# A batched matmul with masked softmax: 16 KB runs over four batches, and the mask in four blocks between the first loads

## The chip, the cores and the metric

The kernel runs on one core of a Trainium2 chip. The metric is the device time of one execution in microseconds. The median of 10 runs of the kernel before is 90.99 us (90.86 to 91.1).

## What is computed

For each of 16 batches a 512x512 matrix x is multiplied by one 512x512 weight matrix, scaled by 0.125, masked and put through a softmax along the rows:

```
y = scale * np.matmul(x, weight)
y = np.where(mask == 1, y, -1e9)
y_exp = np.exp(y - np.max(y, axis=-1, keepdims=True))
out = y_exp / np.sum(y_exp, axis=-1, keepdims=True)
```

The mask is 1 strictly below the diagonal and 0 elsewhere. A row i thus has weight on columns 0 to i-1 alone. Row 0 is masked throughout, so that all its 512 outputs are 1/512. All inputs and the output are fp32: x and the output have 16.8 MB each, the weight and the mask 1 MB each.

## The kernel before

**Units.** The work is cut into 16 units. A unit is one half (h = 0: rows 0 to 255, h = 1: rows 256 to 511) of two neighbouring batches, 512 rows in all. A partition holds four neighbouring rows, 8 KB in one run, so that 64 partitions hold one batch's half, and the two batches alternate from one partition to the next. The line that says it is `x_r = x.rearrange("(c e) (h p t) k -> c h p e (t k)", e=2, h=2, t=T)`, with T = 4. A load or a store moves one unit, 1 MB. Units alternate: even ones are upper halves and need only the first 256 output columns, odd ones need all 512.

**Steps of a unit.** `load` (L80) brings x on SP's queue. `cast` (L85, DVE) makes it bf16. `transpose` (L94, PE) puts 16 blocks of 128x128 into PSUM, and `evict` copies them out, one half on DVE (L104) and one on ACT (L105). `multiply` has, for each of four row slots t, four matmuls with the weight (L118), one matmul that adds the mask band (L127, an identity times a precomputed tile `band`, with -512 at masked places) and an exponential on ACT that also sums the row (L137). `normalise` takes the reciprocal (L152) and scales the rows (L154) on DVE, and for upper halves GpSimd writes 1/512 over row 0 (L156). `store` (L160) is issued on SP's queue. Output tiles of upper halves have their right-hand 256 columns zeroed once, ahead of the loop (L179), as they stay zero; row 0 gets its 1/512 there as well (L180).

**Mask.** Only the four diagonal 128x128 blocks of the mask are read, by one transfer of 256 KB in 512 runs of 512 B (L164). DVE turns them into 0 and -512 (L194). Four matmuls with a spreading matrix (L208) put them on the partitions of the unit layout, and DVE and ACT copy them into `band` (L215). The spreading matrix is made from the identity by ACT (L186), and the constant parts of `band` are filled by GpSimd (L176, L177).

**Order.** Nearly every instruction is inside `seq`, which keeps the order of the program text on each engine. SP's queue starts with load 0, the mask (L164), the weight (L165), and loads 1 to 7 (L167). There are 8 buffers for x and 8 for the output, 3 for xb and 3 for xt. PE first runs 12 dummy matmuls (L173). Then come, in this order, cast 0, the mask's arithmetic, transpose 0, evict 0, the band, the weight's casts (L216, L217) and cast 1. In step u of the loop (L220 on) stand transpose u+1, cast u+2, evict u+1, multiply u, normalise u-1, store u-1 and load u+7; PE thus reaches transpose 1 ahead of multiply 0.

Of the kernel before, what the change touches and what calls it, by code (L numbers as in the profile page):

```python
# [8 lines left out]
FP32 = mybir.dt.float32  # L9
BF16 = mybir.dt.bfloat16  # L10
AF = mybir.ActivationFunctionType
ALU = mybir.AluOpType

MASK_NEG = -512.0
P = 128
X_BUFS = 8
OUT_BUFS = 8
WARM = 12


@with_exitstack
def kernel(
    ctx: ExitStack,
    tc: tile.TileContext,
    x: bass.AP,
    weight: bass.AP,
    scale: float,
    mask: bass.AP,
    out: bass.AP,
):  # L30

    nc = tc.nc

    B, M, K = x.shape
    K2, N = weight.shape
    assert K == K2 and N == 512 and K == 512 and M == 512 and B % 2 == 0
    KT = K // P
    T = 4
    HP = P // 2
    HB = 2 * P
    U = B  # L50

    const = ctx.enter_context(tc.tile_pool(name="const", bufs=1))
    x_pool = ctx.enter_context(tc.tile_pool(name="xf", bufs=X_BUFS))
    xb_pool = ctx.enter_context(tc.tile_pool(name="xb", bufs=3))
    xt_pool = ctx.enter_context(tc.tile_pool(name="xt", bufs=3))
    sum_pool = ctx.enter_context(tc.tile_pool(name="sums", bufs=4))
    psum_t = ctx.enter_context(tc.tile_pool(name="psum_t", bufs=4, space=bass.MemoryType.PSUM))
    psum_y = ctx.enter_context(tc.tile_pool(name="psum_y", bufs=4, space=bass.MemoryType.PSUM))

    x_r = x.rearrange("(c e) (h p t) k -> c h p e (t k)", e=2, h=2, t=T)  # L60
    out_r = out.rearrange("(c e) (h p t) n -> c h p e (t n)", e=2, h=2, t=T)

    diag_r = bass.AP(tensor=mask.tensor, offset=mask.offset, ap=[[N, P], [P * N + P, KT], [1, P]])

    ident_bf = const.tile([P, P], BF16, name="ident_bf")
    w_f32 = const.tile([P, KT, N], FP32, name="w_f32")
    w_bf = const.tile([P, KT, N], BF16, name="w_bf")
    diag_f32 = const.tile([P, KT, P], FP32, name="diag_f32")
    diag_bf = const.tile([P, KT, P], BF16, name="diag_bf")
    spread = const.tile([P, T, P], BF16, name="spread")  # L70
    zeros = const.tile([P, N], BF16, name="zeros")
    band = const.tile([P, 2, T, HB], BF16, name="band")
    ots = [const.tile([P, T, N], FP32, name=f"ot{i}") for i in range(OUT_BUFS)]

    st_x, st_xb, st_pt, st_xt, st_sum = {}, {}, {}, {}, {}
    seq = tc.keep_in_program_order

    def load(u):
        xf = x_pool.tile([P, T, K], FP32, name="xf")
        seq(nc.sync.dma_start(xf.rearrange("p t k -> p (t k)"), x_r[u // 2, u % 2]))  # L80
        st_x[u] = xf

    def cast(u):
        xb = xb_pool.tile([P, T, K], BF16, name="xb")
        seq(nc.vector.tensor_copy(xb, st_x.pop(u)))  # L85
        st_xb[u] = xb

    def transpose(u):
        xb = st_xb.pop(u)
        st_pt[u] = [psum_t.tile([P, 2, T, P], BF16, name="pt") for _ in range(2)]  # L90
        for kt in range(KT):
            for t in range(T):
                seq(
                    nc.tensor.transpose(  # L94
                        st_pt[u][kt // 2][:, kt % 2, t],
                        xb[:, t].rearrange("p (k kt) -> p kt k", kt=KT)[:, kt],
                        ident_bf,
                    )
                )

    def evict(u):
        xt = xt_pool.tile([P, KT, T, P], BF16, name="xt")
        pt = st_pt.pop(u)
        seq(nc.vector.tensor_copy(xt[:, 0:2], pt[0]))  # L104
        seq(nc.scalar.copy(xt[:, 2:4], pt[1]))  # L105
        st_xt[u] = xt

    def multiply(u):
        h = u % 2
        NC = (h + 1) * HB  # L110
        xt = st_xt.pop(u)
        ot = ots[u % OUT_BUFS]
        rsum = sum_pool.tile([P, T], FP32, name="rsum")
        for t in range(T):
            py = psum_y.tile([P, N], FP32, name="py")
            for kt in range(KT):
                seq(
                    nc.tensor.matmul(  # L118
                        py[:, :NC],
                        lhsT=xt[:, kt, t],  # L120
                        rhs=w_bf[:, kt, :NC],
                        start=(kt == 0),
                        stop=(kt == KT - 1),
                    )
                )
            seq(
                nc.tensor.matmul(  # L127
                    py[:, h * HB : NC],
                    lhsT=ident_bf,
                    rhs=band[:, h, t],  # L130
                    start=False,
                    stop=True,
                    skip_group_check=True,
                )
            )
            seq(
                nc.scalar.activation(  # L137
                    out=ot[:, t, :NC],
                    in_=py[:, :NC],
                    func=AF.Exp,  # L140
                    bias=0.0,
                    scale=float(scale),
                    accum_out=rsum[:, t : t + 1],
                )
            )
        st_sum[u] = rsum

    def normalise(u):
        ot = ots[u % OUT_BUFS]
        NC = (u % 2 + 1) * HB  # L150
        rinv = sum_pool.tile([P, T], FP32, name="rinv")
        seq(nc.vector.reciprocal(rinv, st_sum.pop(u)))  # L152
        for t in range(T):
            seq(nc.vector.tensor_scalar_mul(ot[:, t, :NC], ot[:, t, :NC], rinv[:, t : t + 1]))  # L154
        if u % 2 == 0:
            seq(nc.gpsimd.memset(ot[0:2, 0, :HB], 1.0 / N))  # L156

    def store(u):
        ot = ots[u % OUT_BUFS]
        seq(nc.sync.dma_start(out_r[u // 2, u % 2], ot.rearrange("p t n -> p (t n)")))  # L160


    load(0)
    seq(nc.sync.dma_start(diag_f32, diag_r))  # L164
    seq(nc.sync.dma_start(w_f32, weight.rearrange("(p kt) n -> p kt n", kt=KT)))  # L165
    for u in range(1, X_BUFS):
        load(u)  # L167


    nc.vector.memset(zeros, 0.0)  # L170
    idle = psum_y.tile([P, N], FP32, name="py")
    for _ in range(WARM):
        seq(nc.tensor.matmul(idle, lhsT=zeros[:, :P], rhs=zeros, start=True, stop=True))  # L173

    make_identity(nc, ident_bf)
    nc.gpsimd.memset(band[:HP, :, :, P:], MASK_NEG)  # L176
    nc.gpsimd.memset(band[HP:, :, :, :P], 0.0)  # L177
    for i in range(0, OUT_BUFS, 2):
        nc.vector.memset(ots[i][:, :, HB:], 0.0)  # L179
        nc.gpsimd.memset(ots[i][0:2, 0, HB:], 1.0 / N)  # L180


    for g in range(2):
        for e in range(2):
            seq(
                nc.scalar.copy(  # L186
                    spread.rearrange("k t (g p e) -> k t g p e", g=2, e=2)[:, :, g, :, e],
                    ident_bf.rearrange("k (p t) -> k t p", t=T),
                )
            )  # L190

    cast(0)
    seq(
        nc.vector.tensor_scalar(  # L194
            out=diag_bf,
            in0=diag_f32,
            scalar1=-MASK_NEG,
            scalar2=MASK_NEG,
            op0=ALU.mult,
            op1=ALU.add,  # L200
        )
    )
    transpose(0)
    evict(0)
    for t in range(T):
        pm = psum_y.tile([P, N], FP32, name="py")
        seq(
            nc.tensor.matmul(  # L208
                pm, lhsT=spread[:, t], rhs=diag_bf.rearrange("k b c -> k (b c)"), start=True, stop=True
            )  # L210
        )
        for g, copy in enumerate((nc.vector.tensor_copy, nc.scalar.copy)):
            half = slice(g * HP, (g + 1) * HP)
            src = pm.rearrange("p (h g c) -> p h g c", h=2, g=2)
            seq(copy(band[half, :, t, g * P : (g + 1) * P], src[half, :, g]))  # L215
    seq(nc.vector.tensor_copy(w_bf[:, 0:2], w_f32[:, 0:2]))  # L216
    seq(nc.scalar.copy(w_bf[:, 2:4], w_f32[:, 2:4]))  # L217
    cast(1)

    for u in range(U + 1):  # L220
        if u + 1 < U:
            transpose(u + 1)
        if u + 2 < U:
            cast(u + 2)
        if u + 1 < U:
            evict(u + 1)
        if u < U:
            multiply(u)
        if u >= 1:
            normalise(u - 1)  # L230
            store(u - 1)
            if u - 1 + X_BUFS < U:
                load(u - 1 + X_BUFS)


# [33 lines left out]
```

The softmax here doesn't subtract the row's maximum and nothing guards it: scores larger than these inputs give would overflow.

## Time and profile before

| what | value |
|---|---|
| median of 10 runs | 90.99 us (90.86 to 91.1) |
| profiled execution | 91.0 us |
| its span, first to last instruction | 89.2 us |
| mean granted TensorE clock | 0.933 |
| busy: PE, DVE, ACT, POOL | 71.5, 60.4, 55.3, 7.3 us |
| DMA queue of the kernel: packets, MB | 5280, 34.87 |
| time that their packets took, share of 16 engines' span | 94.0% |
| mean over the span | 392 GB/s |
| median time from issue to landing: load, store, weight, mask | 14.1, 10.9, 8.5, 6.6 us |

The profile is that of one execution; its times count from the first instruction. PE is TensorE (PEld its weight loads), DVE is VectorE, ACT is ScalarE, POOL is GpSimd, SP is the engine that issues the transfers. A row of a timeline has the start, the length, the engine, the line and the operation, and in brackets how long the engine was idle before it and what ended that. A table by stretches of time gives for each stretch its length, the busy time of PE, PEld, DVE, ACT and POOL (with the instructions in brackets), the granted clock of TensorE, the mean busy share of the 16 DMA engines (packets are counted where they begin, so it can be a little over 1) and the rate in GB/s. The trace also holds a record of each DMA packet, and of each transfer's landing on each engine.

### The profile page before, as it was taken

What the parts mean: (1) busy time and instruction counts of PE and PEld (TensorE: products, weight loads), DVE (VectorE), ACT (ScalarE), POOL (GpSimd) and SP (SyncE); (2) the same over time, 40 slices, a digit from 0 to 9 for tenths busy, and PEclk for the clock granted to TensorE, in tenths of its full rate; (3) what the DMA queues carried; (4) which work ended last, traced back from release to release, by engine and by line L of the source; (5) the groups of instructions that cost most, each with busy time, mean ns of one, the idle gap of its engine ahead of it and who ended that gap; (6) DMA issues with size and microseconds to landing.
All of it is one profiled execution on the core that took longest, in us unless ns stands there. A gap on an engine that the chain in (4) does not pass through costs nothing.

```text
span 89.2 us, 1618 instructions
## 1 busy us (share of the span) xinstructions
PE 71.5 (80%) x592; PEld 49.2 (55%) x592; DVE 60.4 (68%) x123; ACT 55.3 (62%) x154; POOL 7.3 (8%) x20
## 2 busy tenths in 40 slices
PE   4976305999999999999999999999999999930000
PEld 1325005776598579649847965985697487500000
DVE  5866914758669949986994999599594966525000
ACT  5402930648777869687787877778787778650000
POOL 7620000002000200010020002002000200200000
PEclk9999975569999999999999999999999999999855
DMA  0969999999999999999999999999999999999970
GB/s 0 323 215 369 423 423 445 415 423 423 423 426 415 423 430 434 419 412 430 419 423 430 434 415 423 430 426 426 430 419 419 430 423 430 423 430 423 434 301 22
DMA packets 5286, 34.95 MB, mean 392 GB/s; under 512 B 544, under 2 KB 1056, under 8 KB 1056
## 3 DMA queue, kind: packets, MB, share of 16 engines
q1 hardware_dynamic: 5280, 34.87, 94.0%
q8 instruction: 4, 0.07, 0.3%
q14 instruction: 2, 0.02, 0.0%
HBM read 18.09 MB, written 16.78 MB: 391 GB/s over the span
## 4 chain that ended last, share of the span: by engine, by line
PE 72%; DMA 12%; DVE 3%; SPq 2%; ACT 1%; DVEq 0%; issue 0%; ACTq 0%
PE py L118 48%; PE pt L94 16%; DMA xf<-in_x_dram 12%; PE py L127 8%; DVE ot L154 1%; DVE xb L85 1%; SPq L80 1%; ACT ot L137 1%; SPq L164 1%; SPq L165 1%; DVEq L264 0%; DVE rinv L152 0%; ACTq L264 0%
## 5 line engine op out<-in xcount | busy, mean ns | idle before, releaser
L118 PE MATMUL py<-w_bf,xt 128*128 128x256 bf16 (+1 forms) x256 | 50.9, 333 | 0.0
L137 ACT ACTIVATE ot<-py 128x256 f32<-128x256 f32 (+1 forms) x64 | 31.2, 494 | 8.4 <-PE py L127 8.2
L118 PEld LDWEIGHTS <-xt 128*128 128x128 bf16 x256 | 25.1, 100 | 12.6
L105 ACT COPY xt<-pt 128x1024 bf16<-128x1024 bf16 x16 | 16.2, 1013 | 14.9 <-PE pt L94 10.4
L85 DVE CAST xb<-xf 128x2048 bf16<-128x2048 f32 x16 | 19.5, 1221 | 6.9 <-DMA xf<-in_x_dram 6.9
L154 DVE TENSOR_SCALAR ot<-ot,rinv 128x256 f32<-128x256 f32 (+1 forms) x64 | 23.5, 431 | 0.8
L94 PE MATMUL pt<-ident_bf,xb 128*128 128x128 bf16 x256 | 17.8, 225 | 6.0 <-DVE xb L85 6.0
L94 PEld LDWEIGHTS <-xb 128*128 128x128 bf16 x256 | 16.6, 115 | 7.9 <-DVE xb L85 7.0
L127 PE MATMUL py<-band,ident_bf 128*128 128x256 bf16 x64 | 17.8, 279 | 0.0
L104 DVE COPY xt<-pt 128x1024 bf16<-128x1024 bf16 x16 | 11.0, 688 | 7.8 <-PE pt L94 7.8
L137 ACT ACTIVATION_READ_ACCUMULATOR ot<-py 128x1 f32 x64 | 12.8, 200 | 0.0
L156 POOL MEMSET ot<- 2x256 f32 x8 | 3.6, 449 | 67.3 <-DVE ot L154 67.3
L127 PEld LDWEIGHTS <-ident_bf 128*128 128x128 bf16 x64 | 6.4, 100 | 4.3
L173 PE MATMUL py<-zeros 128*128 128x512 bf16 x12 | 4.9, 595 | 1.2 <-DVE zeros L170 1.2
L152 DVE RECIPROCAL rinv<-rsum 128x4 f32<-128x4 f32 x16 | 2.7, 169 | 3.2 <-ACT ot L137 3.2
L179 DVE MEMSET ot<- 128x1024 f32 x4 | 3.6, 912 | 0.6 <-issue 0.6
L173 PEld LDWEIGHTS <-zeros 128*128 128x128 bf16 x12 | 1.6, 144 | 3.9 <-issue 2.8
L186 ACT ACT_TABLE_LOAD x1 | 1.3, 1283 | 0.7 <-PEq L250 0.7
L215 DVE CAST band<-py 64x256 bf16<-64x256 f32 x4 | 1.4, 406 | 0.0
L215 ACT CAST band<-py 64x256 bf16<-64x256 f32 x4 | 1.3, 368 | 0.0
L180 POOL MEMSET ot<- 2x256 f32 x4 | 1.2, 302 | 1.5 <-DVE ot L179 1.4
L208 PE MATMUL py<-diag_bf,spread 128*128 128x512 bf16 x4 | 1.0, 377 | 0.2 <-DVE diag_bf L194 0.2
(14 smaller groups left out, 6.6 us busy)
## 6 DMA issues: line engine op xcount, KB each, us to landing
xf<-in_x_dram SPq DMA_DIRECT2D x16, 1024.0 KB, 14.1
out_dram<-ot SPq DMA_DIRECT2D x16, 1024.0 KB, 10.9
w_f<-in_weight_dram SPq DMA_DIRECT2D x1, 1024.0 KB, 8.5
diag_f<-in_mask_dram SPq DMA_DIRECT2D x1, 256.0 KB, 6.6
```

Source lines behind the costliest of these rows:

```text
L85: seq(nc.vector.tensor_copy(xb, st_x.pop(u)))
L94: nc.tensor.transpose(st_pt[u][kt // 2][:, kt % 2, t], xb[:, t].rearrange("p (k kt) -> p kt k", kt=KT)[:, kt], ident_bf,)
L104: seq(nc.vector.tensor_copy(xt[:, 0:2], pt[0]))
L105: seq(nc.scalar.copy(xt[:, 2:4], pt[1]))
L118: nc.tensor.matmul(py[:, :NC], lhsT=xt[:, kt, t], rhs=w_bf[:, kt, :NC], start=(kt == 0), stop=(kt == KT - 1),)
L127: nc.tensor.matmul(py[:, h * HB : NC], lhsT=ident_bf, rhs=band[:, h, t], start=False, stop=True, skip_group_check=True,)
L137: nc.scalar.activation(out=ot[:, t, :NC], in_=py[:, :NC], func=AF.Exp, bias=0.0, scale=float(scale), accum_out=rsum[:, t : t + 1],)
L152: seq(nc.vector.reciprocal(rinv, st_sum.pop(u)))
L154: seq(nc.vector.tensor_scalar_mul(ot[:, t, :NC], ot[:, t, :NC], rinv[:, t : t + 1]))
L156: seq(nc.gpsimd.memset(ot[0:2, 0, :HB], 1.0 / N))
L173: seq(nc.tensor.matmul(idle, lhsT=zeros[:, :P], rhs=zeros, start=True, stop=True))
L179: nc.vector.memset(ots[i][:, :, HB:], 0.0)
```

## The change

A group is now one half of four neighbouring batches, 2 MB. A partition holds eight neighbouring rows, a run of 16 KB; 32 partitions hold one batch's half, and four batches alternate. A group has two units: row slots 0 to 3 and 4 to 7. The order of units is therefore two upper, two lower, two upper and so on. There are 5 x buffers and 4 output buffers of 2 MB, and two buffers each for xb and xt.

Group 0 is loaded in two halves of 1 MB (8 KB runs); groups 1 to 7 are loaded whole. Groups 0 and 7 are stored in halves, groups 1 to 6 whole, after their second unit's normalise.

The mask's diagonal blocks come by four transfers of 64 KB, each to 16 partitions with eight neighbouring rows of 512 B. SP's queue starts with: first half of group 0, block 0, weight, block 1, second half of group 0, block 2, group 1, block 3, groups 2 to 4. The band is made in two parts, blocks 0 and 1 ahead of the first multiply, and blocks 2 and 3 after multiply 1; its tile has eight slots. Fourteen more dummy matmuls stand on PE behind transpose 0, and multiply 0 stands ahead of transpose 1.

```
-X_BUFS = 8
-OUT_BUFS = 8
+X_BUFS = 5
+OUT_BUFS = 4
...
-    xb_pool = ctx.enter_context(tc.tile_pool(name="xb", bufs=3))
-    xt_pool = ctx.enter_context(tc.tile_pool(name="xt", bufs=3))
+    xb_pool = ctx.enter_context(tc.tile_pool(name="xb", bufs=2))
+    xt_pool = ctx.enter_context(tc.tile_pool(name="xt", bufs=2))
...
+    x_r = x.rearrange("(c e) (h p t) k -> c h p e (t k)", e=E, h=2, t=S)
+    out_r = out.rearrange("(c e) (h p t) n -> c h p e (t n)", e=E, h=2, t=S)
...
+    def load(g, part=slice(0, S)):
+        if g not in st_x:
+            st_x[g] = x_pool.tile([P, S, K], FP32, name="xf")
+        run = slice(part.start * K, part.stop * K)
+        seq(nc.sync.dma_start(st_x[g].rearrange("p t k -> p (t k)")[:, run], x_r[g // 2, g % 2][:, :, run]))
...
+    def load_diag(b):
+        rows = slice(b * P, (b + 1) * P)
+        seq(
+            nc.sync.dma_start(
+                diag_f32[b * P // S : (b + 1) * P // S],
+                mask[rows, rows].rearrange("(p t) c -> p t c", t=S),
+            )
+        )
...
-    load(0)
-    seq(nc.sync.dma_start(diag_f32, diag_r))
+    load(0, slots(0))
+    load_diag(0)
     seq(nc.sync.dma_start(w_f32, weight.rearrange("(p kt) n -> p kt n", kt=KT)))
-    for u in range(1, X_BUFS):
-        load(u)
+    load_diag(1)
+    load(0, slots(1))
+    load_diag(2)
+    load(1)
+    load_diag(3)
+    for g in range(2, X_BUFS):
+        load(g)
...
     cast(0)
...
     transpose(0)
+    spin(14)
     evict(0)
...
     seq(nc.vector.tensor_copy(w_bf[:, 0:2], w_f32[:, 0:2]))
     seq(nc.scalar.copy(w_bf[:, 2:4], w_f32[:, 2:4]))
+    make_band(0)
     cast(1)
+    multiply(0)
+    transpose(1)
+    evict(1)

     for u in range(U + 1):
-        if u + 1 < U:
+        if 2 <= u + 1 < U:
             transpose(u + 1)
         if u + 2 < U:
             cast(u + 2)
-        if u + 1 < U:
+        if 2 <= u + 1 < U:
             evict(u + 1)
-        if u < U:
+        if 1 <= u < U:
             multiply(u)
+        if u == 1:
+            make_band(1)
         if u >= 1:
             normalise(u - 1)
-            store(u - 1)
-            if u - 1 + X_BUFS < U:
-                load(u - 1 + X_BUFS)
+            g, second = divmod(u - 1, 2)
+            if g in (0, G - 1):
+                store(g, slots(u - 1))
+            elif second:
+                store(g)
+            if second and g + X_BUFS < G:
+                load(g + X_BUFS)
```

`slots(u)` is the slice of row slots of unit u. `make_band(h)` does the mask's arithmetic on its two blocks (32 partitions, 1024 elements each), two matmuls with the spreading matrix, and after each a copy on DVE and one on ACT (64 partitions, 512 elements each). `spin(n)` issues n dummy matmuls of 512 columns.

## The prediction

> **What bounds the kernel now.** I read the page's slices first, then its DMA queues, then the chain. The chain puts 72% on PE, which would make TensorE the bound; the slices say something else.
>
> ```profile
> PE   4976305999999999999999999999999999930000
> DMA  0969999999999999999999999999999999999970
> GB/s 0 323 215 369 423 423 445 415 423 423 423 426 415 423 430 434 419 412 430 419 423 430 434 415 423 430 426 426 430 419 419 430 423 430 423 430 423 434 301 22
> DMA packets 5286, 34.95 MB, mean 392 GB/s; under 512 B 544, under 2 KB 1056, under 8 KB 1056
> q1 hardware_dynamic: 5280, 34.87, 94.0%
> ```
>
> PE is idle in the last four slices while the DMA engines go on at 423 to 434 GB/s. From the fifth slice to the 37th they are full at one rate, whether loads, stores or both are moving. Two early slices (215 and 369) are poor. The packets are 544 semaphore writes (34 transfers x 16 engines), 512 mask rows of 512 B, and 4224 of 8 KB. Next, stretches of time: busy columns first, the last two numbers are DMA share and GB/s.
>
> ```profile
> 5.00:5.50 0.50, 0.50 (x3) 0.21 (x2) 0.43 (x1) 0.00 (x0) 0.01 (x1) 1.00 0.81 324
> 5.50:6.00 0.50, 0.50 (x3) 0.09 (x1) 0.00 (x0) 0.00 (x0) 0.29 (x1) 1.00 0.50 127
> 6.00:6.50 0.50, 0.10 (x1) 0.00 (x0) 0.45 (x1) 0.00 (x0) 0.00 (x0) 1.00 0.50 136
> 6.50:7.00 0.50, 0.00 (x0) 0.00 (x0) 0.50 (x1) 0.00 (x0) 0.00 (x0) 1.00 0.33 54
> 7.00:7.50 0.50, 0.16 (x3) 0.17 (x4) 0.28 (x1) 0.00 (x0) 0.00 (x0) 1.00 0.98 320
> ...
> 70.00:80.00 10.00, 8.86 (x66) 5.60 (x64) 5.83 (x19) 7.40 (x23) 0.90 (x2) 1.00 1.01 426
> 80.00:82.00 2.00, 0.00 (x0) 0.00 (x0) 1.51 (x4) 0.00 (x0) 0.00 (x0) 1.00 1.00 422
> 82.00:84.00 2.00, 0.00 (x0) 0.00 (x0) 0.00 (x0) 0.00 (x0) 0.00 (x0) 1.00 1.02 430
> ```
>
> From 5.4 to 7.2 us the engines move the mask and stand idle half of that time; nowhere else between 3.4 and 85 us is there such a hole. Third, the end and the loads. The last row is the last store; the two casts wait for consecutive 1 MB loads.
>
> ```profile
> 13.07 1.23 DVE L85 CAST xb<-xf 128x2048 bf16<-128x2048 f32 x1 [1.79 <-DMA xf<-in_x_dram]
> 15.55 1.23 DVE L85 CAST xb<-xf 128x2048 bf16<-128x2048 f32 x1 [1.26 <-DMA xf<-in_x_dram]
> ...
> 81.54 0.54 SPq L160 DMA_DIRECT2D out_dram<-ot  x1
> ```
>
> The last store is issued at 81.54 and its landings, one for each engine, run from 86.07 to 88.19. The landings of the store ahead of it run from 83.64 to 85.76, 2.43 us earlier at both ends: each engine went from one to the other without a pause. So **the slowest DMA engine's list of packets sets the end**. A store that met an empty queue would need 81.54 + 1.46 (issue to first packet, from 0.74 to 2.20 for the first load) + 2.43 + 0.75 (receipt) = 86.2. PE, whose last matmul ends at 78.87, thus has 2.0 us to spare.
>
> [...] The trace runs at 423 to 430[...] its packet records have medians of 309 ns for 8 KB, 27 for 512 B and 9 for the semaphore writes, so 282 ns for 7680 B, or 27.2 B/ns, and about 8 ns a packet whatever its size. Check: 8 packets of 309 and one of 9 are 2.48 us, and 15.55 - 13.07 is 2.48. [...] Here it fell at 12.4 us, after PE had nothing from 9.6 on, and came back at 19.2.
>
> **The change, part by part.** The profiled execution took 91.0 us (span 89.2 and 1.8 around it); the median of the runs is 90.99, so one sum serves both.
>
> *16 KB runs.* Each engine carries 8 packets of a load or store. Loads 1 to 7 and stores 1 to 6 become 2 MB with 16 KB runs: 13 x 8 = 104 packets in place of 208. By the fit a packet of 16 KB takes 8 + 16384/27.2 = 610 ns against 618 for two, say 7 to 8 ns saved, 0.75 us per engine. Group 0 and the stores of group 7 stay at 8 KB. [...] the fit has no 16 KB data packet in it, so I allow a loss too, up to +1.7 (16 ns more than two small ones), see the rivals. I take **-0.75**.
>
> *Fewer transfers.* 34 become 24 (9 loads, 10 stores, 4 mask blocks, the weight): 10 semaphore writes of 9 ns per engine, **-0.09**. SP's issue time, about 0.6 us each, is off the path: SP has long waits for the normalise (57.5 us in all) and has issued the first ten transfers by 8.6 us, while their data last until 22. Now the first nine transfers, through the 2 MB load behind the last mask block, are issued by about 6 us.
>
> *Mask in four blocks.* 512 rows of 512 B before and after, 32 per engine, busy 32 x 27 = 0.86 us either way. What can go is the hole: 5.4 to 7.2 us is 1.8 us, so 0.9 idle. Before, 32 small packets follow on each engine; now 8, with a megabyte on either side. Best, the hole is gone, -0.9. Worst, a quarter of it comes back at each block, 0 (a loss beyond that has no ground: the bytes and rows are the same). The records show 512 B packets in two bursts of about 16 per engine with a gap from 6.4 to 6.8 us; 8 are half a burst, so I take **-0.65**.
>
> *Starting order.* Multiply 0 is moved ahead of transpose 1, and the loads of group 1 come as 2 MB. Landings, from the first load's 6.03: block 0 about 6.3, weight 9.0 (before 10.57), block 1 9.3, second half of group 0 11.8, group 1 17.0. The 14 added dummy matmuls sit on PE ahead of the band and multiply 0. At the 0.22 us that a warm 128x512 matmul takes they end at 8.42 + 3.0 = 11.5, some 0.9 us after the band's input is ready: that is their price, covered because PE then waits anyway. Band: two matmuls, then two casts on each of DVE and ACT, twice as wide as the 406 and 368 ns rows, 1.3 us; multiply 0 runs from 12.1 to 14.5; cast 1 is behind the band casts on DVE, 14.3; transpose 1 ends at 15.5. Transpose 2 stands ahead of multiply 1 on PE and needs cast 2, so the 2 MB load: 17.0 + 1.2 = 18.2. PE idles for 2.7 us.
>
> *From there to PE's end.* Units of 256 columns take 0.89 + 2.18 = 3.07 us of PE, of 512 columns 4.77 (chain). From 18.2: 14 transposes at 0.89, seven narrow and eight wide multiplies (15.3 + 31.0), the second band 0.5: 59.3, so 77.5, against 78.87 before. If the clock falls in the wait, add up to 2.4 (half of 12.4 to 19.2 that PE was busy, from 14.36). DVE per narrow unit has 1.22 + 0.69 + 0.17 + 1.27 = 3.35 us, 0.3 more than PE, twice running; the wide units (3.75 of 4.77) give that back, and an eviction has 1 to 2 us before PE needs it. Later loads are early: group 5, issued about 28.4, lands near 42 and is used at 50; group 7 near 62 for use at 65.7.
>
> *Stores.* One 2 MB store for two units leaves up to 4.8 us later than its first half did. Cover: queued work. Store 5 is issued about 65 and the queue holds until 70; store 6 about 71 against 75; the two halves of group 7 at 76 and 80.1 against 81 and 83.6. The last has 83.6 - 80.1 - 1.5 = 2.0 us. Without cover its delay would add one for one. The wider DVE and POOL fills at the start are the same bytes and end before 6 us. Halving xb and xt to two buffers costs nothing: each is read, in PE's order, before its next writer. The dropped x buffers matter no more, as 10 MB are still ahead.
>
> **Sum**: -0.75 - 0.09 - 0.65 = -1.5; 91.0 - 1.5 = **89.5 us**. The slowest engine's last packet then ends near 85.9 in place of 87.4.
>
> **The rivals.** (1) *Only one half works*: runs of 16 KB are as slow as two of 8 KB, 90.3, or the hole comes back block by block, 90.2. For it: no 16 KB data packet was seen, and what limits small packets isn't shown. (2) *Compute takes over.* The mask gains nothing, group 1 lands at 17.9, PE idles for 3.7 us and its clock falls for 4.8: PE ends at 78.4 + 2.4 = 80.8, the last store leaves at 83.5 and lands at 88.1 as before: 90.9. Against: the dummies, and 2.0 us of room. (3) *Slower: 16 KB runs move worse.* Place: each of 104 packets on each engine. Price: 16 ns over two small ones is 104 x 16 = 1.7 us, less 0.74 of the other parts: 91.9. It decides from 7 ns on. For it: the only 16 KB packets in the trace, four of the instruction queue, took 945 to 1024 ns, far over 618, and four batches stand a megabyte apart. Against: those shared their engine with the data queue[...]. (4) *All goes to its best end*: [...] below 88.9 the last store's own path would be the bound.
>
> **How the numbers follow.** A measurement of this kernel tells about 0.2% (0.2 us). Chances: forecast (89.2 to 90.0) 57%, one half 18%, compute 8%, slower 12%, best end 5%. Faster 0.80, same 0.08, slower 0.12. Range 88.9 to 90.9: it leaves out the slower case and part of the compute case.
>
> **What would show it.** Right: no slice under 380 GB/s after the first two; plain rate up one per cent, to about 428 to 430; engines still full when PE has stopped; last store issued near 80. Wrong: DMA share below 0.9 before 83 us (compute), a half-clock stretch at 17 to 22 us, packets over 618 ns, or a dip at each of the four blocks.

## The result, and the profile after

The changed kernel takes 93.51 us (median of 9 runs, 92.31 to 94.17) against 90.98 for the kernel before: a ratio of 1.0225, 95% interval 1.0201 to 1.0249. Slower by 2.2%, where 89.5 was forecast. The ratio leaves out executions more than 1.5% above a kernel's fastest (here two, 93.73 and 94.17), so it is below 93.51 / 90.98 = 1.028, and differences from the changed kernel are taken from the ratios below, 0.01 being 0.91 us. Its profiled execution took 93.62 us with a span of 91.8.

First the page's slices: TensorE, its granted clock, the DMA engines and their rate, and the packets.

```profile
PE   4965968305999999999999999999999999993000
PEclk9999999965589999999999999999999999999955
DMA  0969999999999999999999999999999999999691
GB/s 0 378 189 399 321 360 385 403 340 407 435 421 435 407 417 417 457 421 393 432 439 421 421 357 400 435 435 435 414 435 435 414 414 393 400 428 400 250 417 61
DMA packets 3462, 34.95 MB, mean 381 GB/s; under 512 B 384, under 2 KB 896, under 8 KB 896
```

The packets are as forecast: 384 semaphore writes, and the 8 KB packets mostly gone. The rate is not. From the third slice to the ninth (4.6 to 21 us) 380 GB/s and more were forecast; four of the seven show 189, 321, 360 and 340, where the plain rate is some 425. TensorE has a gap in the eighth slice to the tenth and then half its clock. And near the end there is a slice of 250 GB/s that the kernel before didn't have. The first weakness in steps of half a microsecond (the last two columns are DMA share and GB/s):

```profile
5.00:5.50 0.50, 0.50 (x3) 0.25 (x2) 0.42 (x1) 0.00 (x0) 0.24 (x2) 1.00 1.31 211
5.50:6.00 0.50, 0.49 (x3) 0.00 (x0) 0.00 (x0) 0.00 (x0) 0.28 (x1) 1.00 0.15 58
6.00:6.50 0.50, 0.00 (x0) 0.00 (x0) 0.00 (x0) 0.00 (x0) 0.00 (x0) 1.00 0.40 157
6.50:7.00 0.50, 0.00 (x0) 0.00 (x0) 0.48 (x1) 0.00 (x0) 0.00 (x0) 1.00 0.55 229
...
9.50:10.00 0.50, 0.50 (x4) 0.20 (x2) 0.00 (x0) 0.44 (x1) 0.00 (x0) 1.00 0.83 198
...
12.50:13.00 0.50, 0.50 (x4) 0.14 (x3) 0.26 (x1) 0.00 (x0) 0.00 (x0) 1.00 0.84 219
...
18.00:18.50 0.50, 0.00 (x0) 0.00 (x0) 0.00 (x0) 0.00 (x0) 0.00 (x0) 1.00 1.34 308
18.50:19.00 0.50, 0.00 (x0) 0.00 (x0) 0.00 (x0) 0.00 (x0) 0.00 (x0) 1.00 0.80 214
```

The rows at 5.0 to 6.5, at 9.5, at 12.5 and at 18 to 19 us are the places where a mask block has just passed. Each is a dip in the rate, and the kernel before has only one, though its mask came in one piece of four times the size. But only the first dip is idle time. The table counts a packet where it begins; counted over the packets' whole lengths, the engines are idle for about half of 5.5 to 6.5, and hardly at all in the other three places. There the packets themselves take longer: those of 16 KB that begin between 12 and 14 us have a median of 932 ns, and 611 over the whole run. From 4 to 25 us, each engine spends 2.7 us more in its packets than their usual lengths come to (the run's medians for each size), in the kernel before 0.3. It is idle for 0.7 us there, in the kernel before for 0.9. So most of the loss at the start is slow packets. The expectations below call all four places holes.

What PE makes of it, in the timeline:

```profile
15.85 1.06 PE L98 MATMUL pt<-ident_bf,xb 128*128 128x128 bf16 x16
20.43 2.36 DVE L89 CAST xb<-xf 128x2048 bf16<-128x2048 f32 x2 [3.24 <-DMA xf<-in_x_dram]
21.71 1.90 PE L98 MATMUL pt<-ident_bf,xb 128*128 128x128 bf16 x16 [4.81 <-DVE xb L89]
...
30.16 3.52 SPq L165 DMA_DIRECT2D out_dram<-ot  x2
```

PE finishes transpose 1 at 16.9. Cast 2 needs group 1, which lands at 20.34 on its slowest engine (17.0 was forecast), so PE stands idle for 4.8 us. Its granted clock falls to half at 19.0 and is back at 25.8 (in the kernel before it was at half from 12.4 to 19.2); the 16 transposes at 21.71 take 1.90 us in place of 1.06. The first store goes out at 30.2, in the kernel before at 22.6. The last one leaves at 86.1, as the last start in its row says:

```profile
L165 SPq DMA_DIRECT2D out_dram<-ot x10: 538/548/621, 30.2 to 86.1; - x10
```

That is late enough for the queue to run dry, in the table of stretches at the end:

```profile
85.00:86.00 1.00, 0.00 (x0) 0.00 (x0) 1.00 (x3) 0.00 (x0) 0.00 (x0) 1.00 0.93 385
86.00:87.00 1.00, 0.00 (x0) 0.00 (x0) 0.07 (x1) 0.00 (x0) 0.00 (x0) 1.00 0.33 139
87.00:88.00 1.00, 0.00 (x0) 0.00 (x0) 0.00 (x0) 0.00 (x0) 0.00 (x0) 0.64 0.84 352
88.00:89.00 1.00, 0.00 (x0) 0.00 (x0) 0.00 (x0) 0.00 (x0) 0.00 (x0) 0.50 1.06 434
```

From 86 to 87 the engines are a third busy, then the last 1 MB moves. By the landing records most of the 16 engines waited; the slowest went from the last store but one (landed at 88.56) to the last (91.01) in 2.45 us, without a pause. The last landing stands 0.36 us behind the end of the last packet (90.65), in the kernel before 0.47 (88.19 behind 87.72), where the forecast had 0.75 for the receipt. So two things end together here: PE's work, and the list of the slowest DMA engine.

### The profile page after: what moved, and what is told of

The parts are those of the page before. It is cut to its first block, busy times and chain, and to the rows that moved or that the text cites. A ratio compares the mean times of both kernels' runs of the same rounds, so it can differ in the third digit from the quotient of the medians.

```text
span 91.8 us, 1619 instructions
## 1 busy us (share of the span) xinstructions
PE 74.6 (81%) x606; PEld 50.1 (55%) x606; DVE 61.8 (67%) x122; ACT 56.0 (61%) x154; POOL 6.6 (7%) x14
## 4 chain that ended last, share of the span: by engine, by line
PE 67%; DMA 17%; SPq 4%; DVE 3%; ACT 1%; issue 1%; DVEq 0%; ACTq 0%
PE py L122 44%; DMA xf<-in_x_dram 17%; PE pt L98 15%; PE py L131 7%; SPq L172 2%; DVE ot L158 1%; SPq L85 1%; DVE xb L89 1%; ACT ot L141 1%; SPq L181 1%; PE py L226 1%; DVEq L305 0%; DVE rinv L156 0%; ACTq L305 0%; DVEq L89 0%
## 5 line engine op out<-in xcount | busy, mean ns | idle before, releaser
L109 ACT COPY xt<-pt 128x1024 bf16<-128x1024 bf16 x16 | 16.2, 1013 | 15.7 <-PE pt L98 11.5
L158 DVE TENSOR_SCALAR ot<-ot,rinv 128x256 f32<-128x256 f32 (+1 forms) x64 | 23.0, 423 | 0.7
L89 DVE CAST xb<-xf 128x2048 bf16<-128x2048 f32 x16 | 19.5, 1221 | 4.8 <-DMA xf<-in_x_dram 4.8
L196 PE MATMUL py<-zeros 128*128 128x512 bf16 x26 | 8.0, 473 | 1.2 <-DVE zeros L191 1.2
L160 POOL MEMSET ot<- 4x256 f32 x4 | 1.8, 448 | 66.8 <-DVE ot L158 66.8
L196 PEld LDWEIGHTS <-zeros 128*128 128x128 bf16 x26 | 2.9, 117 | 5.3 <-issue 2.7
L237 DVE CAST band<-py 64x512 bf16<-64x512 f32 x4 | 2.6, 678 | 3.5 <-PE py L226 3.5
L204 DVE MEMSET ot<- 128x2048 f32 x2 | 3.5, 1765 | 0.8 <-issue 0.8
L237 ACT CAST band<-py 64x512 bf16<-64x512 f32 x4 | 2.3, 582 | 2.0 <-DVE band L237 2.0
L247 DVE CAST w_bf<-w_f 128x1024 bf16<-128x1024 f32 x1 | 0.7, 695 | 1.8 <-DMA w_f<-in_weight_dram 1.8
L202 POOL MEMSET band<- 64x2048 bf16 x1 | 1.8, 1801 | 0.1
L201 POOL MEMSET band<- 64x2048 bf16 x1 | 1.8, 1803 | 0.0
```

The lines of the kernel that those rows point to most:

```text
L89: seq(nc.vector.tensor_copy(xb, st_x[u // 2][:, slots(u)]))
L237: copy(band[half, h, slots(j), g * P : (g + 1) * P], pm.rearrange("p (t c) -> p t c", t=T)[half],)
```

## The experiments

I held three theories. **A**: each short mask transfer opens a hole in the DMA queue, which delays all that follows. **B**: PE's order is at fault, as transpose 2 waits for a whole 2 MB load and the clock falls. **C**: 16 KB runs over four batches are served worse. Numbers in brackets are ratios to the kernel before, with 95% intervals.

### The mask left out (e1)

```
-        seq(nc.sync.dma_start(diag_f32[...], mask[rows, rows]...))
+        if b == 0:
+            nc.gpsimd.memset(diag_f32, 1.0)
```

> The changed kernel without its four mask transfers (the blocks are filled with ones on GpSimd, so the mask is left out of the computation). Theory A (each 64 KB block opens a hole of about 1 us in the DMA queue; that delays every engine's list and group 1): no slice under 380 GB/s after the first two, group 1 lands near 17 us, the engines' spread at the start falls below 1 us, PE ends near 78, about 90.0 us. Rival B (compute order: transpose 2 waits for a whole 2 MB load, and the clock falls): PE still waits over 4 us at half clock, 92.5. Rival C (16 KB runs over four batches drive the engines apart): rate and spread as in the changed kernel, 92.3 or more.

90.43 us (0.995, 0.9925 to 0.9975): 2.5 us less than with the mask, by the ratios. Group 1 lands at 15.67 with the engines within 0.4 us, PE waits 1.5 us for it, the clock stays up, and the first store leaves at 23.9.

```profile
17.35 1.08 PE L98 MATMUL pt<-ident_bf,xb 128*128 128x128 bf16 x16 [1.47 <-DVE xb L89]
23.86 3.50 SPq L165 DMA_DIRECT2D out_dram<-ot  x2
```

Rival C is out: with the same 16 KB runs the spread at the start is gone. The cause lies with the four transfers, a quarter of a megabyte out of 35.

### Group 1 in halves (e2), and the clock kept up (e3)

```
-    load(1)
-    load_diag(3)
+    load(1, slots(0))
+    load_diag(3)
+    load(1, slots(1))
```

> The changed kernel with group 1 loaded as two transfers of 1 MB, block 3 between them. Theory A: unit 2 can start some 2 us earlier, but the slowest DMA engine's list is as long as before, so 93.0 to 93.5. Rival B (PE's start sets the time): PE ends near 81, about 91. Rival C: 93.5.

```
     transpose(1)
+    spin(20)
     evict(1)
```

> The changed kernel with 20 more dummy matmuls behind transpose 1, which keep TensorE's clock up while it waits for group 1. Theory A: PE ends about 2 us earlier, near 81.5, but the slowest engine's list stays, 93.0 to 93.4. Rival B: the clock was the loss, 91.5. Rival C: 93.5.

e2 took 92.26 us (1.0149, 1.0084 to 1.0213), e3 91.73 (1.0087, 1.0066 to 1.0108). Each was less than A had said and more than B had, e3 only by a little. In e3 the clock never falls while work is left:

```profile
PEclk9999999999999999999999999999999999999555
```

Both undo a consequence, and each gets back part. In e2 PE ends at 79.2 and the last store leaves at 81.9, 4.2 us earlier than in the changed kernel, yet it lands only 1.2 us earlier, at 89.79: there the slowest engine's list is the end. So neither A nor B alone: the blocks lengthen the DMA list, and by way of group 1 they start PE late and cold. Either one holds the end up when the other is mended.

### The kernel before with four blocks (e4)

```
-    seq(nc.sync.dma_start(diag_f32, diag_r))
+    seq(nc.sync.dma_start(diag_f32[:, 0:1], diag_r[:, 0:1]))
     seq(nc.sync.dma_start(w_f32, ...))
+    (block 1, load 1, block 2, load 2, block 3)
```

> The kernel before with its mask in four transfers of 64 KB (one diagonal block each, on 128 partitions), the first second in the queue, then one behind the weight, one behind load 1 and one behind load 2; all else is the kernel before. Theory A: three more holes of about 1 us at the start, 93 to 94. Rivals B and C: nothing of theirs is in it, 90.5 to 91.0.

94.60 us (1.0388, 1.035 to 1.0425), a little more than A had said. But the trace shows another reason, so this supports nothing. All four blocks gate this kernel's band, and the fourth lands at 15.04: DVE waits 8 us for it, and the first store leaves at 26.9.

```profile
15.16 0.43 DVE L203 TENSOR_SCALAR diag_bf<-diag_f 128x512 bf16<-128x512 f32 x1 [7.97 <-DMA diag_f<-in_mask_dram]
26.94 0.61 SPq L160 DMA_DIRECT2D out_dram<-ot  x1
```

Meanwhile the clock is down. The stores come late, so that the queue is empty from 27 to 28 us, where no packet begins; the rate stays uneven until 40:

```profile
PEclk9999965556999999999999999999999999999855
GB/s 28 308 404 361 358 418 421 436 418 432 414 202 340 290 436 358 305 382 436 407 439 407 443 421 418 421 436 421 428 428 414 439 411 439 414 432 414 390 315 21
```

And where A expected three more holes there are none: load 3 lands at 17.49, in the kernel before at 18.02. These blocks have the same bytes and the same runs of 512 B as those of the changed kernel. What differs is where they land: 128 partitions with one row each, in place of 16 partitions with eight.

### What in a block opens the hole (e5, e6, e8)

e5 keeps place and size of the blocks but moves 4 KB runs, to 16 partitions (mask left out); e6 issues the real blocks on ACT's queue; e8 is the changed kernel again.

```
+        seq(nc.sync.dma_start(side[b], mask[32 * b : 32 * b + 32].rearrange("(p t) c -> p (t c)", t=2)))
```

> The changed kernel with each of its four mask transfers replaced by one of the same 64 KB at the same place in the queue, but in 16 runs of 4 KB in place of 128 runs of 512 B; they go to a tile that nothing reads, and the blocks are filled with ones on GpSimd (so the mask is left out of the computation). Theory A1 (any short transfer opens the hole[...]): holes as before, 92.5 to 93.5. Theory A2 (the 512 B runs are what is slow): about the kernel without the mask plus 0.6 us for 256 KB, 91.0.

```
-            nc.sync.dma_start(
+            nc.scalar.dma_start(
```

> The changed kernel with its four mask transfers issued on ACT's queue in place of SP's, all at the start. Theory A1: beside the loads on SP's queue they open no hole between loads; only their packets cost time, 91.0 to 91.4. Theory A2: the 512 B runs cost the same on any queue, 92.5 to 93.5.

> The changed kernel once more, unaltered, for a second profile beside the others of this batch. If the holes vary from run to run, group 1 lands anywhere from 18.3 us (as with the added dummies) to 20.4 (as in the first profile), and the time goes with it, 92.3 to 94.2; if the dummies had a hand in the early landings, 20 us and 93.5 again.

e5: 92.57 us (1.0174, 1.0155 to 1.0192), group 1 at 18.80. So it isn't the 512 B runs. e6: 92.39 (1.0148, 1.0104 to 1.0191), group 1 at 19.17. So it isn't the place in SP's queue either; on ACT's queue the blocks trickle in beside the loads for up to 17 us:

```profile
DMA to landing us min/median/max: 6.3/10.5/17.1
```

e8: 92.82 (1.0198, 1.0154 to 1.0241), group 1 at 19.15. What the blocks cost varies from run to run, so that single profiles of this kernel differ by more than a microsecond; the earlier landing in e3 (18.35) may be more of the same. A1, that any short transfer does it, still stood after these three, but e4 spoke against it.

### The kernel before without its mask (e7)

```
-    seq(nc.sync.dma_start(diag_f32, diag_r))
+    nc.gpsimd.memset(diag_f32, 1.0)
```

> The kernel before without its mask transfer (blocks filled with ones on GpSimd, the mask left out of the computation). It gives the price of the mask in the kernel before and, against the changed kernel without its mask (90.4), what the rest of the change is worth. If the mask cost 1.8 us there, 89.2, and the rest of the change loses 1.2. If runs of 16 KB pay as forecast (0.75), 91.2 would have to come out, which leaves the mask no price at all; in between, the rest of the change is worth the difference.

90.33 us (0.9928, 0.9905 to 0.9951). Load 3 lands 1.9 us earlier (16.10), but only 0.65 arrives at the end. The rate falls short while the last of the first loads are under way (the first store is issued at 19.5, the second at 23.5 us):

```profile
24.00:25.00 1.00, 1.00 (x13) 0.65 (x11) 1.00 (x2) 0.54 (x2) 0.00 (x0) 1.00 1.10 295
25.00:26.00 1.00, 1.00 (x7) 0.52 (x6) 0.96 (x5) 1.00 (x3) 0.28 (x1) 1.00 0.88 320
```

The engines are not idle there; over their whole length the packets fill these two microseconds. Again they take longer: of the 75 packets of 8 KB that begin there 26 take over 430 ns, where 309 is usual. With that the slowest engine falls back: one load lands from 22.90 to 24.66 on the 16 engines, the next from 25.83 to 28.61. At the end the first engine is done 1.4 us earlier than in the kernel before (84.70 against 86.07), the slowest only 0.7 (87.49 against 88.19). So a gain in the first loads isn't all kept: the slowest engine's lag takes a part of it, and my sum had no such term. Why packets slow down there isn't shown; e1 has the same from 27 to 31 us, 1.2 us per engine.

Against e1 (90.43 us, 0.995) this run also prices the rest of the change: without the mask it is worth nothing, where 0.84 us had been forecast for it.

### Where the blocks land (e9, e10)

Both leave the mask out and move its blocks, at their places, to a tile that nothing reads.

```
e9:  nc.sync.dma_start(side[b], mask[rows, rows])
e10: nc.sync.dma_start(side[b][::8], mask[rows, rows].rearrange("(p t) c -> p t c", t=S))
```

> The changed kernel with its four mask transfers replaced by four of the same bytes (128 runs of 512 B, same place in the queue) that go to 128 partitions with one row each, in place of 16 partitions with eight rows each. They go to a tile that nothing reads, and the blocks are filled with ones on GpSimd (the mask is left out of the computation). Theory D (what opens the hole is that a block lands on 16 neighbouring partitions[...]): blocks cost 0.35 us each, group 1 lands at 16.5 to 17.0 with the engines within 1 us, 90.5 to 91.0. Theory A1 (any short transfer): group 1 at 18.5 to 20, 92.5.

> As the kernel with 128 partitions (mask left out likewise), but each block goes to 16 partitions that lie eight apart, with eight rows each. Theory D: [...] less than half of the excess, group 1 at 17.0 to 17.8, 91 to 92. Theory A1, or a theory in which it is the eight rows to a partition: as in the changed kernel, group 1 at 18.5 or later, 92.5.

e9: 90.99 us (0.9993, 0.9978 to 1.0008), group 1 at 17.61. e10: 92.08 (1.0137, 1.0102 to 1.0173), group 1 at 18.47. With 16 neighbouring partitions it is 92.57 with the mask left out likewise (e5), 93.51 and 92.82 with it. Same bytes, same places in the queue, equally short: that a block is short (A1) is not the cause of the excess. Theory D, the place where a block lands, holds for 128 partitions in the time, though group 1 comes 0.6 us later than it said. For 16 spread ones, where "less than half of the excess" was my estimate, the order is right, but the times don't decide: e10 lies just beyond the slow end of what D said, its range (91.84 to 92.83) touches that of the neighbours (from 92.31), and the rival with eight rows to a partition had put group 1 at 18.5.

The lengths of the packets separate them better. From 4 to 25 us they exceed the usual, per engine, by 2.7, 1.9 and 2.4 us with 16 neighbours (the changed kernel, e8, e5), by 1.3 with 16 spread partitions (e10), by 0.6 with 128 (e9; also e11 and e12), and by 0.2 with no block at all (e1). As e10 has as many partitions, and as many rows to each, as the changed kernel, how far apart they lie matters by itself (1.3 us against 1.9 to 2.7), as far as single profiles tell.

From e10 to e9 the number of partitions changes along with their distance, and no run here shows what it is in the place that makes the packets longer.

### The blocks on 128 partitions, with the whole computation (e11, e12, e13)

```
-                diag_f32[b * P // S : (b + 1) * P // S],
-                mask[rows, rows].rearrange("(p t) c -> p t c", t=S),
+                diag_f32[:, b : b + 1], mask[rows, rows]...
...
-        for j in range(2):
+        for t in range(S):
             ... lhsT=spread[:, t], rhs=diag_bf[:, 2 * h : 2 * h + 2] ...
```

> The changed kernel with each mask block loaded to 128 partitions, a row to each, at the same places in the queue, and the band made from that (eight matmuls of 256 columns and sixteen casts of 128 columns in each half). The computation is whole. Theory D: group 1 lands near 16.7, PE waits about 2 us less than in the changed kernel, PE ends near 79, 90.7 to 91.4. Theory A1: 92.5 or more.

e12 and e13 add `spin(10)` behind transpose 1.

> The same with ten more dummy matmuls behind transpose 1, so that the clock cannot fall while PE waits for group 1. Theory D: the wait is short enough without them, so within 0.3 us of the kernel without the ten, 90.5 to 91.2. Theory A1: 91.7, as the changed kernel with dummies.

> The kernel with 128-partition mask blocks and ten dummies again, as the measure for the two others: 90.3 to 90.7, under the kernel before by 0.4 to 0.6 us.

e11: 90.98 us (1.0004, 0.9982 to 1.0025). e12: 90.49 (0.9954, 0.9934 to 0.9974), e13: 90.53 (0.9948, 0.993 to 0.9965). Behind the first block of e12 there is no hole, and group 1 lands at 17.12, where the prediction had it at 17.0 (17.59 in e11, whose own expectation was 16.7):

```profile
5.00:6.00 1.00, 1.00 (x4) 0.30 (x2) 0.50 (x2) 0.77 (x3) 0.52 (x2) 1.00 1.00 361
6.00:7.00 1.00, 0.42 (x2) 0.00 (x0) 1.00 (x1) 0.00 (x0) 0.00 (x0) 1.00 1.01 426
```

```profile
17.21 2.36 DVE L89 CAST xb<-xf 128x2048 bf16<-128x2048 f32 x2 [0.68 <-DMA xf<-in_x_dram]
18.50 1.08 PE L98 MATMUL pt<-ident_bf,xb 128*128 128x128 bf16 x16
```

PE, which has the dummies to do, hardly waits for group 1, and the clock and the DMA engines stay up to the end:

```profile
PEclk9999999999999999999999999999999999999955
DMA  1999999999999999999999999999999999999760
GB/s 15 339 376 373 374 427 420 428 420 443 428 421 450 395 421 402 457 450 413 428 450 413 398 443 413 421 457 398 428 435 413 443 428 428 428 413 424 332 288 15
```

The ten dummies are worth 0.5 us, which e12's expectation had not granted them: in e11 the clock still fell at 18.2 for 3.4 us. e12 is the fastest whole kernel of this study, 0.4 to 0.5 us under the kernel before.

### The two forecast gains by themselves (e14, e15)

Both start from e12. e14 makes every 2 MB transfer two of 1 MB with 8 KB runs; e15 brings the mask as one transfer of 256 KB, second in the queue.

```
e14: -        load(g)
     +        load(g, slots(0)); load(g, slots(1))          (stores likewise)
e15: -    load_diag(0)                                      (and no load_diag(1) to (3))
     +    seq(nc.sync.dma_start(diag_f32, bass.AP(..., ap=[[N, P], [P * N + P, KT], [1, P]])))
```

> The same, but every 2 MB load and store is two transfers of 1 MB with runs of 8 KB, issued one after the other; buffers, order and all else are as in the kernel with 16 KB runs. If a packet of 16 KB saves 7 to 8 ns over two and the DMA list sets the end: 13 x 8 x 7.5 ns plus 13 semaphore writes, 0.8 to 0.9 us slower than the measure, 91.3. If the end is set by PE's late start: no difference, or faster, as group 1 comes in halves and unit 2 can start 1.5 us earlier, 90.0 to 90.5.

> The same as the measure, but with the mask in one transfer of 256 KB in second place, as in the kernel before. If the hole of that transfer (0.9 us idle) is what four blocks save: group 1 lands 0.5 to 0.9 us later, 90.9 to 91.4. If four blocks of this shape cost as much as the one: 90.3 to 90.7.

e14: 91.21 us (1.0027, 1.0014 to 1.0039). The runs of 16 KB, with the fewer semaphore writes, are worth 91.21 - 90.53 = 0.68 us; 0.75 and 0.09 had been forecast. Its packets are those of an 8 KB kernel:

```profile
DMA packets 5336, 34.97 MB, mean 391 GB/s; under 512 B 592, under 2 KB 1104, under 8 KB 1104
```

e15: 90.99 us (1.0008, 0.9992 to 1.0023). Four blocks in place of one are worth 0.46, where 0.65 was forecast, and e15's profile has the hole:

```profile
5.00:6.00 1.00, 0.81 (x4) 0.19 (x2) 0.56 (x2) 0.78 (x3) 0.52 (x2) 1.00 0.39 105
6.00:7.00 1.00, 0.00 (x0) 0.00 (x0) 1.00 (x1) 0.00 (x0) 0.00 (x0) 1.00 0.36 92
```

## Why the prediction was wrong

**The step that failed** is the bound on the mask's four blocks: "Worst, a quarter of it comes back at each block, 0 (a loss beyond that has no ground: the bytes and rows are the same)". The loss beyond that is what came. Bytes and rows were the same; the partitions were not. The diff says so (16 partitions with eight rows each, before 128 with one), and I had listed it in the change without giving it a price. Group 1 lands at 15.67 without a mask, at 17.1 to 17.6 behind three blocks on 128 partitions, and at 18.4 to 20.3 behind three on 16 neighbours: 0.5 to 0.6 us a block against 0.9 to 1.6. In the time, by the ratios, the shape with the band's arithmetic that goes with it is 2.0 us against e11 (1.8 in the repeat), as much as the whole slowdown. And what the blocks cost is mostly not the idle hole that the bound counted, but longer packets of the loads beside them (2.7 us per engine; 0.6 in e11).

**The terms that held.** A 16 KB packet takes 611 ns (610 forecast), and e14 finds 0.68 of the 0.84 us in the time. Four blocks for one save 0.46 of the forecast 0.65, once they land widely. The two don't add up at the end, though: e13 has both, 1.1 us together, and is only 0.5 under the kernel before; and without the mask (e1 against e7) the rest of the change gains nothing. The sum let the slowest engine's list shrink like the others'. In e12 the store ahead of the last lands on the first engine 1.05 us earlier than in the kernel before (82.59 against 83.64), on the slowest 0.2 (85.56 against 85.76); this lag of 3.0 us in place of 2.1 had no term in the sum. The rival of 16 KB runs that move worse is thus refuted. The 14 dummies end at 11.9 (11.5 forecast). The halved buffers cost nothing that shows: no wait for a free buffer of xb, xt or the output stands in the list of waits.

**The rival that came nearest** is the second, compute takes over: PE's wait for group 1, the fallen clock and the empty queue at the end all happened. Its size was off for the same reason. It put group 1 at 17.9, and 20.34 came; it put PE's end at 80.8, and 83.4 came. From transpose 2 to PE's end were forecast 59.3 us plus up to 2.4 for the clock; 61.7 were measured, so this part of the sum held. I had let that rival end at 90.9 because its only source of delay was a mask that gains nothing. That blocks could lose, and that the loss would then be paid twice (list and start), was in no case of mine; the 12% for slower stood for 16 KB runs that move worse. Two of the signs listed for being wrong did come, a dip at each block and a half-clock stretch (19.0 to 25.8 us).

**Where the time went**, by the runs: between the changed kernel and e13 lie 2.5 us, by the ratios. With the clock kept up (e3) about half of them, 1.3 us, is gone (1.0 against the repeat); the shape of the blocks costs the other half, from e3 to e13. They are not quite separate, as e3 has 20 dummies and e13 ten.

**What stays open.** Why packets slow down beside a block on 16 partitions (932 ns in place of 611 for 16 KB, from 12 to 14 us), why the loss varies from run to run, and why packets slow down in e1 and e7 where no block is near, isn't shown.

## What to carry to other kernels

Price a transfer by where it lands as well as by its bytes and runs: three blocks on 16 neighbouring partitions delayed what followed by 2.7 to 4.7 us, the one transfer with all their bytes on 128 partitions (e15) by 2.2, and three blocks on 128 by 1.5 to 1.9. When a bound is called one-sided, look for what the edit changes besides the thing that is counted. When a rate falls, ask whether the engines are idle, as behind the one mask transfer of e15, or their packets are longer, as beside most of the blocks here. When the slowest engine sets the end, look at its lag besides the mean work (3.0 us in e12, 2.1 in the kernel before). A queue that looks full all along has a second condition, that the first stores are ready when the first loads end (e4 fails it at 27 us); and a wait of PE at the start can be paid again in clock (1.0 to 1.3 us here).

## What the runs showed that I had not expected

- Four transfers of 64 KB, 0.7% of the bytes, took 2.5 us (e1), and their rows of 512 B had no part that shows (e5).
- Small transfers on a second queue did not slip in between: they were up to 17 us on the way, and the loads beside them were as late (group 1 at 19.17) as with the blocks in the same queue (e6).
- Taking the mask out of the kernel before brings the loads 1.9 us forward and the end 0.65 (e7).
- By the packet records of the two kernels, each 16 KB packet of the instruction queues took 0.88 to 1.09 us. At some of them the slowest engine's lag grows: in the kernel before from 0.6 to 1.7 us at 24 us, in the changed kernel from 1.4 to 3.0 at 41; at others (38 us before, 26 us after) it doesn't. That the fetches are the cause isn't shown.
